# Ranking two experts with the router's tiles, searching for the other fourteen between weight tiles, and pinning the order of the expert units

## The chip, the cores and the metric

The kernel runs on one core of a Trainium2 chip. The metric is device microseconds (us) of one execution. Before the change the median of three runs is 1372.27 us (1369.42 to 1372.28).

## What is computed

One block of a hybrid diffusion transformer: 1024 latent tokens of width 1024 (and 256 context tokens that give a start state) go through a gated linear attention and a long convolution, and then through a mixture of experts in which each expert chooses its tokens. Only the last part is touched:

```
def _ec_moe(h, w_router, w_gate, w_up, w_down):      # 16 experts, cap = 128 tokens each
    aff = jax.nn.softmax((h @ w_router).astype(jnp.float32), axis=-1)
    vals, idx = lax.top_k(jnp.swapaxes(aff, 1, 2), cap)
    xs = h[bidx, idx]
    hid = jax.nn.silu(xs @ w_gate) * (xs @ w_up)      # per expert, 1024 x 1024 weights
    y = (hid @ w_down) * vals[..., None]
    return jnp.zeros_like(h).at[bidx, idx].add(y)
```

## The kernel before, in words

The program is one long function; a scheduling layer orders the instructions of each engine when the program is built, and each engine then runs its own list in that order. The stages up to the residual are not touched. The last two are:

**Router.** For each of the eight tiles of 128 tokens (tile 7 first, tile 0 last) the kernel finishes the attention output (`gla_out`), multiplies by the output weights (`residual`, matmuls into `pout`) and computes the 16 affinities (`router`: transposes `pth`, matmuls `plt`, softmax, the result in `aff`, line 1214). GpSimd (POOL) writes the tile to `d_acc` and the normed tile to `d_h`.

**Experts.** Each expert needs the places of its 128 best tokens. `select` (line 1273) finds the threshold by a search over the 30 bits of the affinity: a step makes candidate thresholds `thr` on VectorE (DVE), compares all affinities with them (`ge`, line 1309), lets TensorE (PE) count over the partitions (`psel`, line 1283, eight matmuls against a matrix of ones) and keeps the largest candidate with at least 128 tokens above it (lines 1314 and 1315). After the last step ties are resolved (`gt`, `eq`, `keep`) and `pos` holds each token's place. `select` is called twice: for experts 0 and 1 with 6 steps of 5 bits (names end in `a`), for experts 2 to 15 with 15 steps of 2 bits (names end in `b`). The second call is written behind `route(1)` and the scheduler spreads it over the first weight tiles.

`route(e)` (line 1347) turns places into token numbers: a one-hot `oh` on DVE, eight small matmuls into `pi`, a copy and an addition give `ix`, and POOL gathers the 128 rows of `d_h` into the single buffer `xs` (line 1362). `transposed` (line 1366) transposes those rows (`ptx` on PE), applies the norm's gain on ScalarE (ACT, `tt`) and splits them into a high and a low part, `thi` on ACT and `tlo` on DVE.

A **unit** is one 1024 x 1024 weight matrix: eight tiles `eraw` (or `erawl` for `w_down`), each split by ACT into `ehi` (line 144) and by DVE into `elo` (line 147), and each multiplied by six matmuls of 512 columns into `pex` (lines 150 to 152: high x high, low x high, high x low, for two halves). The units run gate 0, up 0, gate 1, down 0, up 1, gate 2, down 1 and so on. Expert e's gate ends with a silu on ACT (line 1385, `sg`), its up with a product on DVE (line 1406, `sg` again), its down with the scaled rows `y` on DVE (line 1417), which POOL adds into `d_acc`. `next_rows` transposes the next expert's rows and routes the one after it, behind tile 2 of an up unit (`KU`), and the hidden rows of the expert before are transposed behind tile 5 of a gate unit (`KB`); the scheduler may move all of these. The weight tiles are loaded by SyncE (SP) into 21 buffers for gate and up and 8 for down; `elo` has 4 buffers and `ehi` 5.

Of the kernel before, what the change touches and what calls it, by code (L numbers as in the profile page):

```python
# [42 lines left out]
def shape_constants():  # L43
# [45 lines left out]
    out["tokid"] = tid  # L89
    for b in (5, 2):  # L90
# [8 lines left out]
def tile_gla_hyena_moe(ctx: ExitStack, tc: tile.TileContext, io: dict, out: bass.AP):  # L99
# [49 lines left out]
    def mm3(out_, lh, ll, rh, rl, first, last):  # L149
        T.matmul(out_, lh, rh, start=first, stop=False)  # L150
        T.matmul(out_, lh, rl, start=False, stop=False)  # L151
        T.matmul(out_, ll, rh, start=False, stop=last)  # L152

# [821 lines left out]
    def gb(tag, bufs):  # L975
        return lambda shape, name: psg.tile(shape, F32, name=name, tag=tag, bufs=bufs)

    ga, gc, gd, ge1 = gb("ga", 2), gb("gc", 2), gb("gd", 1), gb("ge", 1)

# [119 lines left out]
    tokid = cload("tokid", [P, NT, 2], pool=keep)  # L1099
    digit = {b: cload(f"digit{b}", [P, 30 // b, 1 << b], I32, pool=keep) for b in (5, 2)}  # L1100
    ones = keep.tile([P, P], BF16, name="ones")
# [3 lines left out]
    SY.dma_start(befr, io["c_before"])  # L1105
    V.tensor_copy(before, befr)
    ws = [wout_tile(k, op_tile) for k in range(4)]
    p2a.close()
    g2 = p2.enter_context(tc.tile_pool(name="g2", bufs=1, side="right", reuse_waits="tile"))

    def h4(shape, name, tag, bufs, dt=F32):
        return g2.tile(shape, dt, name=name, tag=tag, bufs=bufs)


# [100 lines left out]

    outs, rows = [], []
    for i in reversed(range(-2 - 1, NT)):
        if i >= 0:
            outs.append((i, gla_out(i)))
        if rows:  # L1220
            router(*rows.pop(0))
        if outs and (i < 0 or len(outs) > 1):
            o_ = outs.pop(0)
            rows.append((o_[0], *residual(*o_)))
    p2.close()
    st_stack.close()
# [7 lines left out]
    def mt(shape, dt, name, tag, bufs):  # L1234
        return mp.tile(shape, dt, name=name, tag=tag, bufs=bufs)
# [5 lines left out]
    used = [0]  # L1241
    KB, KU = 5, 2
# [12 lines left out]

    loaded = {(w, k): expert_tile(w, 0, k) for w in ("w_gate", "w_up", "w_down") for k in range(KT)}

    def expert_mm(w, e, xt, between=None, at=KB):
        ps = pse.tile([P, D], F32, name="pex", tag="ex", bufs=3)
        for k in range(KT):  # L1260
            raw = loaded[w, k] if e == 0 else expert_tile(w, e, k)
            hi = mt([P, D], F32R, "ehi", "ehi", NHI)
            lo = mt([P, D], F32R, "elo", "elo", NLO)
            split(hi, lo, raw)
            for h in range(2):
                hs = slice(h * 512, (h + 1) * 512)
                mm3(ps[:, hs], xt[0][:, k], xt[1][:, k], hi[:, hs], lo[:, hs], k == 0, k == KT - 1)
            if between and k == at:
                between()
        return ps  # L1270

    pos = mp.tile([P, E, NT], BF16, name="pos")

    def select(e0, ne, tag, bits):
# [14 lines left out]

        if e0 == 0:  # L1290
            def pr(n):
                return pT([P, n], "psel")
        else:
            acc = pse.tile([P, D], F32, name="psel", tag="ex", bufs=3)
            flip = [0]

            def pr(n):
                flip[0] ^= 512
                return acc[:, flip[0]:flip[0] + n]

# [3 lines left out]
        for b in range(30 // bits):  # L1304
# [3 lines left out]
            ge = tl([P, nd - 1, ne, NT], BF16, "ge")  # L1308
            V.tensor_tensor(ge, aff_[:, None].to_broadcast([P, nd - 1, ne, NT]),
                            thr[:, 1:nd, :, None].to_broadcast([P, nd - 1, ne, NT]), op=ALU.is_ge)  # L1310
            pc = pr((nd - 1) * ne)
            column_sums(pc, ge.rearrange("p q e t -> p (q e) t"))
            upper = thr[:, 1:nd].rearrange("p q e -> p (q e)")
            V.scalar_tensor_tensor(upper, pc, float(CAP) - 0.5, upper, op0=ALU.is_ge, op1=ALU.mult)
# [6 lines left out]
        pg_ = pr(ne)  # L1321
        column_sums(pg_, gt)
        need = tl([P, ne], F32, "need")
        V.tensor_scalar(need, pg_, -1.0, float(CAP), op0=ALU.mult, op1=ALU.add)
# [9 lines left out]

    NF = 2
    select(0, NF, "a", 5)

# [10 lines left out]
    def route(e):  # L1348
        pi = pT([P, 5], "pi")
        oh = mt([P, NT, P], BF16, "oh", "s2", NS)  # L1350
        V.tensor_tensor(oh, slot[:, None, :].to_broadcast([P, NT, P]),
                        pos[:, e, :, None].to_broadcast([P, NT, P]), op=ALU.is_equal)
        for t in range(NT):
# [27 lines left out]

    def gate_part(e, xt, between=None):
        pg = expert_mm("w_gate", e, xt, between)
        sg = mt([P, D], F32, "sg", "sg", 1)
        A.activation(sg, pg, AF.Silu)
        return sg

    A.preload_act_table_set("silu_and_others")
    routed = [route(0)]
    xt = transposed(0, routed[0][2], True)  # L1390
    routed.append(route(1))
    select(NF, E - NF, "b", 2)
    with tc.issue_after(routed[0][3].ins):
        sg = gate_part(0, xt)
    m5 = row_of(5, mp)
    for e in range(E):
        ahead = []

        def next_rows():
            if e + 1 < E:  # L1400
                ahead.append(transposed(e + 1, routed[e + 1][2], True))
            if e + 2 < E:
                routed.append(route(e + 2))

        pu = expert_mm("w_up", e, xt, next_rows, KU)
        V.tensor_mul(sg, pu, sg)
        if e + 1 < E:
            sg_next = gate_part(e + 1, ahead[0], lambda: ahead.append(transposed(e, sg)))
        else:
            ahead = [None, transposed(e, sg)]  # L1410
        xt_next, ht = ahead
        py = expert_mm("w_down", e, ht)
        iv, ix = routed[e][0:2]
        if e + 1 == E:
            break
# [4 lines left out]
        xt, sg = xt_next, sg_next  # L1420

# [56 lines left out]
```

## Time and profile before

| | us |
|---|---|
| median of three runs | 1372.27 |
| profiled execution, its own time | 1373.86 |
| span of its trace | 1372.1 |
| PE busy in the span | 1277.9 (93%) |
| DVE busy | 1148.6 (84%) |
| ACT busy | 805.4 (59%) |
| expert matmuls into `pex`, number | 2304 |

The profile comes from one profiled execution, 1.59 us above the median; 1.76 us lie around its span. A row of a timeline has a start, a duration, the engine, the line of the kernel, the operation, the tile written and the tiles read; behind it, in brackets, the engine's idle time in front of it and what ended it. PEclk is the granted clock of TensorE as a share of full speed. A matmul's duration overlaps the next one's, so PE's pace is read from the distance of starts.

### The profile page before, as it was taken

Reading aid. Unit: us, or ns where it says so; the run is one execution under the profiler, and the core shown is the slowest. Engines: PE = TensorE matmul, PEld = TensorE weight load, DVE = VectorE, ACT = ScalarE, POOL = GpSimd, SP = SyncE. Lnnn points to the kernel's source line nnn. Section 1 sums busy time; section 2 is a strip of 40 time slices with the busy share of each in tenths; the row PEclk is TensorE's granted clock in tenths of the full one; section 3 lists DMA queues with packets and bytes.
Section 4 is the critical chain, followed back from the end, with each engine's and each line's share of the span. In section 5 each row is a group of like instructions: output and inputs, shape, how many; then the busy total and the mean of one; then the engine's idle time right before and its main releaser. Section 6 shows DMA issues by size and latency. Waiting matters only on the chain.

```text
span 1372.1 us, 21492 instructions
## 1 busy us (share of the span) xinstructions
PE 1277.9 (93%) x7721; PEld 1044.9 (76%) x7721; DVE 1148.6 (84%) x1913; ACT 805.4 (59%) x1226; POOL 126.8 (9%) x136
## 2 busy tenths in 40 slices
PE   6998999999999997998996899999999999999983
PEld 4788877787899896666774678888888888877762
DVE  7899549899767878788656799999999999988886
ACT  3285352211211315785563678888888888877864
POOL 1110000010110110001010000001111111012010
PEclk9999999999999997999996899999999999999996
DMA  8965442775565535666668789999999999999856
GB/s 268 342 195 172 139 108 77 229 187 183 142 201 151 141 113 177 168 159 191 242 227 326 251 322 357 361 393 382 388 389 384 388 389 386 370 374 364 279 184 245
DMA packets 143978, 354.81 MB, mean 259 GB/s; under 512 B 17925, under 2 KB 63629, under 8 KB 143615
## 3 DMA queue, kind: packets, MB, share of 16 engines
q1 hardware_dynamic: 124553, 293.88, 59.7%
q0 software_dynamic: 18928, 59.56, 15.8%
q8 instruction: 60, 0.98, 0.3%
q14 instruction: 47, 0.39, 0.1%
q10 hardware_dynamic: 390, 0.00, 0.0%
HBM read 310.89 MB, written 50.89 MB: 264 GB/s over the span
## 4 chain that ended last, share of the span: by engine, by line
PE 70%; issue 9%; DVE 8%; ACT 6%; DMA 5%; POOL 1%; POOLq 0%; SPq 0%; DVEq 0%; ACTq 0%
PE pex L151 13%; PE pex L152 12%; PE pex L150 12%; PE phy L565 3%; PE phy L563 3%; PE phy L562 3%; PE ptx L1372 2%; PE pdft L487 2%; DMA wt<-w_ada 2%; PE pdft L488 2%; PE pvg L150 2%; PE pvg L151 1%; PE pvg L152 1%; PE pm L351 1%; PE pdft L698 1%
## 5 line engine op out<-in xcount | busy, mean ns | idle before, releaser
L147 DVE TENSOR_TENSOR elo<-eraw,ehi 128x1024 fp32r<-128x1024 f32 x256 | 302.3, 1219 | 13.2 <-issue 6.0
L151 PE MATMUL pex<-elo,thi 128*128 128x512 f32 x768 | 306.0, 398 | 4.8 <-DVE elo L147 4.5
L150 PE MATMUL pex<-ehi,thi 128*128 128x512 f32 x768 | 305.4, 398 | 2.3 <-ACT thi L144 1.3
L152 PE MATMUL pex<-ehi,tlo 128*128 128x512 f32 x768 | 303.2, 395 | 0.8 <-DVE tlo L147 0.8
L144 ACT ACTIVATE ehi<-eraw 128x1024 fp32r<-128x1024 f32 x256 | 265.1, 1068 | 50.2 <-PE pex L152 48.2
L151 PEld LDWEIGHTS pex<-elo,thi 128*128 128x128 f32 x768 | 145.1, 189 | 40.6 <-DVE elo L147 10.7
L150 PEld LDWEIGHTS pex<-ehi,thi 128*128 128x128 f32 x768 | 145.3, 189 | 34.1 <-ACT thi L144 1.7
L152 PEld LDWEIGHTS pex<-ehi,tlo 128*128 128x128 f32 x768 | 145.1, 189 | 31.5 <-DVE tlo L147 1.2
L147 DVE TENSOR_TENSOR elo<-erawl,ehi 128x1024 fp32r<-128x1024 f32 x128 | 149.4, 1218 | 6.3 <-ACT ehi L144 5.5
L144 ACT ACTIVATE ehi<-erawl 128x1024 fp32r<-128x1024 f32 x128 | 131.4, 1057 | 19.7 <-PE pex L152 18.0
L144 ACT ACTIVATE whi<-wraw 128x1024 fp32r<-128x1024 f32 x30 | 31.7, 1058 | 116.5 <-PE pqk L563 28.8
L562 PE MATMUL phy<-xh,whi 128*128 128x512 f32 x192 | 76.7, 399 | 0.0
L563 PE MATMUL phy<-xl,whi 128*128 128x512 f32 x192 | 75.8, 395 | 0.0
L150 PE MATMUL pvg<-whi,xh 128*128 128x256 f32 x256 | 73.2, 286 | 0.0
L151 PE MATMUL pvg<-wlo,xh 128*128 128x256 f32 x256 | 72.4, 283 | 0.0
L152 PE MATMUL pvg<-whi,xl 128*128 128x256 f32 x256 | 72.4, 283 | 0.0
L1418 POOL DMA_INDIRECT d_acc<-y,ix x15 | 34.7, 2313 | 392.3 <-DVE y L1417 392.3
L1377 ACT ACTIVATE tt<-ptx,fcol,gfcol 128x128 f32<-128x128 f32 x128 | 48.7, 463 | 34.0 <-PE ptx L1372 34.0
L565 PE MATMUL phy<-xh,wlo 128*128 128x512 f32 x192 | 61.6, 398 | 1.0 <-DVE wlo L147 1.0
L458 ACT ACTIVATE D<-pdft 128x512 f32<-128x512 f32 x32 | 19.1, 597 | 69.5 <-PE pdft L488 39.0
L147 DVE TENSOR_TENSOR wlo<-wraw,whi 128x1024 fp32r<-128x1024 f32 x30 | 36.7, 1222 | 27.4 <-ACT whi L144 27.4
L487 PE MATMUL pdft<-kk,fmat 128*128 128x128 f32 x256 | 51.4, 283 | 3.2 <-ACT D L458 3.1
(459 smaller groups left out, 2596.2 us busy)
## 6 DMA issues: line engine op xcount, KB each, us to landing
eraw<-w_gate SPq DMA_DIRECT2D x128, 512.0 KB
eraw<-w_up SPq DMA_DIRECT2D x128, 512.0 KB
erawl<-w_down SPq DMA_DIRECT2D x128, 512.0 KB
wt<-w_ada SPq DMA_DIRECT2D x48, 512.0 KB
wraw<-w_in SPq DMA_DIRECT2D x30, 512.0 KB
kspec<-d_spec SPq DMA_DIRECT2D x16, 512.0 KB
xt<-x SPq DMA_DIRECT2D x8, 512.0 KB
d_spec<-ue POOLq DMA_DIRECT2D x8, 512.0 KB, 3.4
```

The source lines that it names most:

```text
L144: A.activation(hi, src, AF.Copy)
L147: V.tensor_sub(lo, src, hi.bitcast(F32))
L150: T.matmul(out_, lh, rh, start=first, stop=False)
L151: T.matmul(out_, lh, rl, start=False, stop=False)
L152: T.matmul(out_, ll, rh, start=False, stop=last)
L487: T.matmul(ps[:, r], fmat[:, r, m1], kk[m1 // 4][:, 0, m1 % 4], start=True, stop=False)
L488: T.matmul(ps[:, r], fneg[:, n1] if r else fmat[:, 0, n1], kk[n1 // 4][:, 1, n1 % 4], start=False, stop=True)
L562: T.matmul(ps[:, h], hi[:, k], rh[k][:, h], start=k == 0, stop=False)
L563: T.matmul(ps[:, h], hi[:, k], rl[k][:, h], start=False, stop=False)
L565: T.matmul(ps[:, h], lo[:, k], rh[k][:, h], start=False, stop=k == KT - 1)
L1377: A.activation(tt[:, k], pt[:, k], AF.Identity, bias=fcol[:, 0, kk_:kk_ + 1], scale=gfcol[:, kk_:kk_ + 1])
L1418: G.indirect_dma_start(out=d_acc[:, :], out_offset=bass.IndirectOffsetOnAxis(ap=ix[:, :1], axis=0), in_=y, in_offset=None, compute_op=ALU.add)
```

## The change

Experts 0 and 1 no longer have a search. As each router tile is done, `rank` transposes the affinities of an expert into a row (`prow`, copied to `arow`), counts on DVE how many tokens of the tiles done so far are above each token of this tile (`over`, with its sum in `cnt`, over 128 elements for tile 7 and up to 1024 for tile 0) and how many equal ones stand ahead (`tie`), and adds both to the rank `rk`. `rank_sums` takes the column sums of `over` on PE (`pbelow`, one small matmul for each tile done earlier) off the ranks of those tiles. At tile 0 the places `pos0` are read off. The rank of tile i is written one tile late, so that tile 1's and tile 0's follow each other; for tile 0, expert 1 comes behind the routing of expert 0.

The search for experts 2 to 15 is a generator that stops after each count. Three steps run ahead of the first unit, the rest are called behind weight tiles listed in `SEARCH_AT`; `route(2)` follows the last.

The units are one sequence: `split_ahead` issues the high parts four tiles and the low parts three tiles ahead of the matmuls, and everything else is put behind the splits and matmuls of its tile (`behind_splits`). The rows of the next expert are transposed behind tile 3 of an up unit, the routing comes behind tile 7, the hidden rows are transposed behind tile 2 of a gate unit. The first `w_down` is loaded by POOL behind the first gather, and the seven of the 21 buffers that lie in another pool are now taken last.

```diff
-        if (used[0] - 1) % (NR + NX) < NX:
+        if (used[0] - 1) % (NR + NX) >= NR:
...
+    def rank(i, experts, ptile, new):
+        W = (NT - i) * P
+        for e in experts:
+            row = ptile([P, P], name="prow")
+            T.transpose(row, aff[:, e, i:i + 1].to_broadcast([P, P]), ident)
+            V.tensor_copy(arow[e][:, i * P:(i + 1) * P], row)
+            a_ = aff[:, e, i:i + 1]
+            over = over2[e][:, i % 2]
+            cnt = tiny.tile([P, 2], F32, name="cnt")
+            V.tensor_scalar(over[:, 0:W], arow[e][:, i * P:], a_, 0.0, op0=ALU.is_gt, op1=ALU.add, accum_out=cnt[:, 0:1])
+            tie = new([P, P], BF16, name="tie")
+            V.scalar_tensor_tensor(tie, arow[e][:, i * P:(i + 1) * P], a_, after, op0=ALU.is_equal, op1=ALU.mult,
+                                   accum_out=cnt[:, 1:2])
+            V.scalar_tensor_tensor(rk[:, e, i:i + 1], cnt[:, 0:1], cnt[:, 1:2], rk[:, e, i:i + 1], op0=ALU.add, op1=ALU.add)
+            overs[e].append((e, i, over))
+            while len(overs[e]) > (i > 0):
+                rank_sums(*overs[e].pop(0), ptile)
+
+    def rank_sums(e, i, over, ptile):
+        if i + 1 < NT:
+            below = ptile([P, NT], name="pbelow")
+            for t in range(i + 1, NT):
+                T.matmul(below[:, t:t + 1], over[:, (t - i) * P:(t - i + 1) * P], ones[:, 0:1], start=True, stop=True)
+            V.tensor_sub(rk[:, e, i + 1:], rk[:, e, i + 1:], below[:, i + 1:])
+        if i == 0:
+            V.scalar_tensor_tensor(pos0[:, e], rk[:, e], CAP + 0.5, rk[:, e], op0=ALU.is_le, op1=ALU.mult)
...
-    select(0, NF, "a", 5)
...
+    def split_ahead(t):
+        while len(his) <= min(t + AH, len(stream) - 1):
...
+            last_split[0] = A.activation(hi, raw, AF.Copy)
...
+        while len(los) <= min(t + AL, len(stream) - 1):
...
+            last_split[1] = V.tensor_sub(lo, raw, hi.bitcast(F32))
...
+    def unit(j, xt, hooks):
+        ps = pse.tile([P, D], F32, name="pex", tag="ex", bufs=3)
+        for k in range(KT):
+            t = KT * j + k
+            split_ahead(t)
...
+            if k in hooks:
+                with behind_splits():
+                    hooks[k]()
...
+    SEARCH_AT = ((0, 1, 2, 4, 6), (0, 2, 5, 7), (1, 3, 5, 7), (0,))
+    search = select(NF, E - NF, "b", 2)
+    rank(0, [1], pT, lambda shape, dt, name: mt(shape, dt, name, "s2", NS))
+    with tc.issue_after(routed[0][4].ins):
+        loaded.update({("w_down", k): expert_tile("w_down", 0, k, G) for k in range(KT)})
...
+    for _ in range(3):
+        next(search)
...
+    def search_step():
+        if next(search, True):
+            routed.append(route(2))
```

Where the instructions now stand, engine by engine. First DVE at the end of the long search, up to the routing of expert 2 (`keepb` and `pos` close the search, `sg` is the product that waits for the end of an up unit, `oh`, `pv` and `ix` are the routing). Before, this lies among the splits of gate 1, and the product at the end of up 0 is long done:

```order
L1329 TENSOR_TENSOR keepb<-keepb,eqb 128x112
L147 TENSOR_TENSOR elo<-eraw,ehi 128x1024
L1330 TENSOR_TENSOR keepb<-keepb,gtb 128x112
L147 TENSOR_TENSOR elo<-eraw,ehi 128x1024
L1333 SCALAR_TENSOR_TENSOR pos<-psel,keepb 128x112
L147 TENSOR_TENSOR elo<-eraw,ehi 128x1024
L1351 TENSOR_TENSOR oh<-slot,pos 128x1024
```

and now, with 43 splits ahead of it, which is three tiles into gate 2:

```order
L1356 TENSOR_TENSOR keepb<-keepb,eqb 128x112
L1426 TENSOR_TENSOR elo<-eraw,ehi 128x1024
L1357 TENSOR_TENSOR keepb<-keepb,gtb 128x112
L1510 TENSOR_TENSOR sg<-pex,sg 128x1024
L1360 SCALAR_TENSOR_TENSOR pos<-psel,keepb 128x112
L1426 TENSOR_TENSOR elo<-eraw,ehi 128x1024
L1376 TENSOR_TENSOR oh<-slot,pos 128x1024
L1382 COPY pv<-pi 128x5
L1383 TENSOR_TENSOR ix<-pv 128x1
```

What moved: the routing of expert 2 stands behind the product of up 1 instead of ahead of it.

Second, PE where the rows of expert 2 are transposed (`ptx<-ident,xs`). Before, 210 expert matmuls (35 weight tiles) are ahead of it, and the eight matmuls `pi` of its routing stand 80 expert matmuls earlier:

```order
L152 MATMUL pex<-ehi,tlo 128x512
L1372 MATMUL ptx<-ident,xs 128x128 x8
L150 MATMUL pex<-ehi,thi 128x512
L151 MATMUL pex<-elo,thi 128x512
```

and now, with 240 expert matmuls (40 tiles, the end of up 1) ahead of it:

```order
L1379 LDWEIGHTS oh
L1379 MATMUL pi<-tv,oh 128x5
L1397 MATMUL ptx<-ident,xs 128x128 x8
L151 MATMUL pex<-ehi,thi 128x512
L152 MATMUL pex<-elo,thi 128x512
```

What moved: no expert matmul is left between the routing of expert 2 and the transposes of the rows that it gathers. The counts of the 12 search steps that are left for the units stand 3, 6, 9, 10, 13, 15, 18, 21, 24, 28, 32 and 35 whole tiles into the sequence, where `SEARCH_AT` calls the last of them 23 tiles in; the tie resolution follows at 38 to 40.

Third, DVE in every later expert, from an up unit's end to the hidden rows of the next gate unit. Before:

```order
L147 TENSOR_TENSOR elo<-eraw,ehi 128x1024
L147 TENSOR_TENSOR tlo<-tt,thi 128x512
L147 TENSOR_TENSOR elo<-eraw,ehi 128x1024
L1406 TENSOR_TENSOR sg<-pex,sg 128x1024
L147 TENSOR_TENSOR elo<-eraw,ehi 128x1024 x6
L147 TENSOR_TENSOR elo<-erawl,ehi 128x1024 x2
L147 TENSOR_TENSOR tlo<-ptx,thi 128x512 x2
```

and now:

```order
L148 TENSOR_TENSOR tlo<-tt,thi 128x512
L1426 TENSOR_TENSOR elo<-eraw,ehi 128x1024
L1376 TENSOR_TENSOR oh<-slot,pos 128x1024
L1510 TENSOR_TENSOR sg<-pex,sg 128x1024
L1382 COPY pv<-pi 128x5
L1426 TENSOR_TENSOR elo<-eraw,ehi 128x1024
L1383 TENSOR_TENSOR ix<-pv 128x1
L1385 TENSOR_REDUCE iv<-pv 128x1
L1426 TENSOR_TENSOR elo<-eraw,ehi 128x1024 x2
L148 TENSOR_TENSOR tlo<-ptx,thi 128x512 x2
```

What moved: three splits instead of eight lie between the product and the hidden rows' low parts, and the one-hot stands directly ahead of the product.

## Rows read from the trace of the kernel before

**Rows 1.** Windows: stretch and its length, then busy time of each engine, PEclk, DMA.

```profile
726.50:731.50 5.00, 1.83 (x22) 1.05 (x23) 1.69 (x12) 4.45 (x11) 1.04 (x2) 0.85 1.03 418
726.00:763.00 37.00, 17.56 (x185) 14.78 (x183) 26.30 (x93) 11.11 (x21) 2.34 (x3) 0.55 0.77 305
842.00:1195.00 353.00, 352.93 (x1683) 288.53 (x1682) 339.36 (x341) 302.60 (x369) 36.51 (x20) 1.00 1.01 383
1195.00:1310.00 115.00, 110.96 (x500) 87.25 (x499) 101.42 (x99) 88.09 (x111) 14.71 (x5) 0.99 0.87 317
```

**Rows 2.** Timeline of ACT: the silu at the end of gates 2, 12 and 15.

```profile
842.29 1.03 ACT L1385 ACTIVATE sg<-pex 128x1024 f32<-128x1024 f32 x1 [0.34 <-PE pex L152]
...
1195.14 1.03 ACT L1385 ACTIVATE sg<-pex 128x1024 f32<-128x1024 f32 x1 [0.31 <-PE pex L152]
...
1309.61 1.03 ACT L1385 ACTIVATE sg<-pex 128x1024 f32<-128x1024 f32 x1 [2.70 <-PE pex L152]
```

**Rows 3.** Timeline of DVE: last affinities, and places of experts 0 and 1.

```profile
731.23 0.29 DVE L1214 TENSOR_SCALAR aff<-ex,sm 128x16 f32<-128x16 f32 x1
...
751.29 0.17 DVE L1333 SCALAR_TENSOR_TENSOR pos<-psel,keepa 128x16 bf16<-128x16 f32 x1
```

**Rows 4.** Timeline of POOL: the gather for expert 0.

```profile
754.42 1.27 POOL L1362 DMA_INDIRECT xs<-d_h,ix  x1 [22.89 <-PE psel L1283]
```

**Rows 5.** Timeline of PE: the first expert matmuls.

```profile
759.74 1.94 PE L1372 MATMUL ptx<-ident,xs 128*128 128x128 f32 x8 [5.73 <-DMA xs<-d_h,ix]
...
764.59 0.77 PE L152 MATMUL pex<-ehi,tlo 128*128 128x512 f32 x1
765.16 0.63 PE L150 MATMUL pex<-ehi,thi 128*128 128x512 f32 x1
...
766.44 0.63 PE L150 MATMUL pex<-ehi,thi 128*128 128x512 f32 x1
...
768.05 0.40 PE L150 MATMUL pex<-ehi,thi 128*128 128x512 f32 x1
...
772.25 0.77 PE L1283 MATMUL psel<-geb,ones 128*128 128x42 bf16 x8
772.82 0.48 PE L150 MATMUL pex<-ehi,thi 128*128 128x512 f32 x1
```

**Rows 6.** DVE groups by form: a scalar operation on 512 elements.

```profile
L246 DVE TENSOR_SCALAR sn<-sy 128x512 f32<-128x512 f32 x2 | 0.8, 422 | 0.0
```

**Rows 7.** Timeline of PE: transposes of a router tile, and one routing.

```profile
699.27 1.09 PE L1197 MATMUL pth<-ident,xres 128*128 128x128 f32 x8
...
801.89 0.36 PE L1354 MATMUL pi<-tv,oh 128*128 128x5 bf16 x8
```

**Rows 8.** DVE groups by form, 900 to 1000 us.

```profile
L147 DVE TENSOR_TENSOR elo<-eraw,ehi 128x1024 fp32r<-128x1024 f32 x46 | 54.4, 1220 | 2.6 <-issue 1.2 <-PE pex L151 0.7
...
L147 DVE TENSOR_TENSOR tlo<-ptx,thi 128x512 fp32r<-128x512 f32 x6 | 3.8, 679 | 0.0
...
L1406 DVE TENSOR_TENSOR sg<-pex,sg 128x1024 f32<-128x1024 f32 x3 | 3.7, 1219 | 0.0
```

**Rows 9.** Timeline of DVE: the product at the end of up 1.

```profile
830.65 1.21 DVE L1406 TENSOR_TENSOR sg<-pex,sg 128x1024 f32<-128x1024 f32 x1
```

**Rows 10.** The tile xs: all sixteen gathers, from issue to landing.

```profile
DMA to landing us min/median/max: 4.7/8.1/12.7
```

**Rows 11.** Timeline of DVE around the product at the end of an up unit.

```profile
1074.51 1.23 DVE L147 TENSOR_TENSOR elo<-eraw,ehi 128x1024 fp32r<-128x1024 f32 x1
1075.65 0.68 DVE L147 TENSOR_TENSOR tlo<-tt,thi 128x512 fp32r<-128x512 f32 x1
1076.25 1.22 DVE L147 TENSOR_TENSOR elo<-eraw,ehi 128x1024 fp32r<-128x1024 f32 x1
1077.42 1.23 DVE L1406 TENSOR_TENSOR sg<-pex,sg 128x1024 f32<-128x1024 f32 x1
```

More of the change, by code (lines that the diff above doesn't have):

```diff
@@ L83, in shape_constants @@
     out["before"] = (ss < cc).astype(f)
+    out["after"] = (ss > cc).astype(f)
     out["slot"] = np.broadcast_to(np.arange(1, P + 1, dtype=f), (P, P)).copy()
@@ L151, in mm3 @@
         T.matmul(out_, lh, rl, start=False, stop=False)
-        T.matmul(out_, ll, rh, start=False, stop=last)
+        return T.matmul(out_, ll, rh, start=False, stop=last)
     def rsqrt(dst, ssum, n, width, fused=False):
@@ L1099, in tile_gla_hyena_moe @@
     tokid = cload("tokid", [P, NT, 2], pool=keep)
-    digit = {b: cload(f"digit{b}", [P, 30 // b, 1 << b], I32, pool=keep) for b in (5, 2)}
+    digit = {b: cload(f"digit{b}", [P, 30 // b, 1 << b], I32, pool=keep) for b in (2,)}
     ones = keep.tile([P, P], BF16, name="ones")
@@ L1106, in tile_gla_hyena_moe @@
     V.tensor_copy(before, befr)
+    after = keep.tile([P, P], F32, name="after")
+    SY.dma_start(after, io["c_after"])
+    pos0 = keep.tile([P, NF, NT], BF16, name="pos0")
+    rk = keep.tile([P, NF, NT], F32, name="rk")
+    V.tensor_scalar(rk, tokid[:, None, :, 1].to_broadcast([P, NF, NT]), 1.0, None, op0=ALU.add)
     ws = [wout_tile(k, op_tile) for k in range(4)]
@@ L1112, in h4 @@
         return g2.tile(shape, dt, name=name, tag=tag, bufs=bufs)
+    arow = [g2.tile([P, L], F32, name="arow0"), mid_tile("arow1")]
+    over2 = [mid.tile([P, 2, L], BF16, name="over", tag="x", bufs=NX) for _ in range(NF)]
     diag = [g2.tile([P, NH, P], F32, name=f"diag{x}") for x in range(2)]
@@ L1220, in tile_gla_hyena_moe @@
         if rows:
+            ranks.append(rows[0][0])
             router(*rows.pop(0))
@@ L1224, in tile_gla_hyena_moe @@
             rows.append((o_[0], *residual(*o_)))
+        while len(ranks) > 1 or ranks == [0]:
+            rank(ranks[0], range(NF if ranks[0] else 1), gc, s2)
+            ranks.pop(0)
     p2.close()
@@ L1254, in expert_tile @@
         return raw
[L1256 to L1270, printed above, removed]
+    loaded = {(w, k): expert_tile(w, 0, k) for w in ("w_gate", "w_up") for k in range(KT)}
     pos = mp.tile([P, E, NT], BF16, name="pos")
@@ L1380, in transposed @@
         return hi, lo
[L1382 to L1386, printed above, removed]
+    units = [("w_gate", 0)]
+    for e in range(E):
+        units += [("w_up", e)] + ([("w_gate", e + 1)] if e + 1 < E else []) + [("w_down", e)]
+    stream = [(w, e, k) for w, e in units for k in range(KT)]
+    AH, AL = NHI - 1, NLO - 1
+    his, los, last_split = [], [], [None, None, None]
@@ new lines, in behind_splits @@
+    def behind_splits():
+        stack = ExitStack()
+        for x in last_split:
+            stack.enter_context(tc.issue_after(x.ins))
+        return stack
+    def unit(j, xt, hooks):
[3 more added lines that the diff above has]
+            split_ahead(t)
+            for h in range(2):
+                hs = slice(h * 512, (h + 1) * 512)
+                last_split[2] = mm3(ps[:, hs], xt[0][:, k], xt[1][:, k], his[t][0][:, hs], los[t][:, hs], k == 0, k == KT - 1)
+            if k in hooks:
+                with behind_splits():
+                    hooks[k]()
+        return ps
@@ L1393, in tile_gla_hyena_moe @@
-    with tc.issue_after(routed[0][3].ins):
-        sg = gate_part(0, xt)
+    for _ in range(3):
+        next(search)
     m5 = row_of(5, mp)
[L1396 to L1412, printed above, removed]
+    sgs, hts = {}, {}
```

79 lines of the change are left out of this document (59 added, 20 removed).

## The prediction

> **What bounds it now.** I read the windows first. From 842 to 1195 us PE is busy 352.9 of 353 us at full clock, DVE 96% [rows 1]: the experts are bound by PE. The silu at a gate's end marks a period: ten experts from 842.29 to 1195.14 take 35.3 us each, the last three up to 1309.61 take 114.5, that is 8.6 more than three regular ones [rows 2]. The reader should see PE at 111 of 115 us there, and DMA below 1 [rows 1]. The second place with idle PE is the border between router and experts: 17.6 of 37 us busy, granted clock 0.55 [rows 1]. There the chain runs from the last affinities at 731.5 through the first search to the places at 751.3 [rows 3], the gather at 754.4 [rows 4], its rows at 759.7, and full work from 764.6, when the first low part of the rows is there [rows 5]. So two gains are in reach: some 20 us of search at the border, and 8.6 us at the irregular end.
>
> **Prices.** PE: between 768.05 and 772.25 lie 18 expert matmuls, 0.233 us each, a tile of six 1.40; a count of the search takes 0.57 (772.25 to 772.82); at the lower clock a matmul takes 0.43 (three from 765.16 to 766.44) [rows 5]. A transpose is 0.11 to 0.14 and eight routing matmuls 0.36 [rows 7]. DVE: a split takes 1.22 by itself and 1.13 to 1.14 in a row of splits [rows 11], a `tlo` 0.6 to 0.68, a product 1.22 [rows 8].
>
> **1. Router stage: 5.9 us later.** Of the 16 `prow` transposes and 56 `pbelow` matmuls, 10 and 12 stand ahead of the last `pout`: about 1.5 us of PE that was full there; I take 2. More costly is DVE. The ranks of tiles 2 and 1 stand between the links of tile 0's own chain (norm, softmax), for two experts each: four `over` of 768 or 896 elements, four copies, four `tie` and eight additions. `over` with its sum is in no row. Its floor is the scalar operation on 512 elements, 0.42 [rows 6], its ceiling a whole 1024-element product, 1.22 [rows 8]; I take 1.0, twice the floor for twice the elements plus a short instruction to read the sum. That makes 4 + 0.8 + 1 + 1.4 = 7.2 us. DVE is idle 3.3 of the 5 us of that chain [rows 1], so 3.9 stick out (2 to 6 with the bounds). The affinities end at 737.4.
>
> The Trainium skill (VectorE: DVE Perf Modes, The perf-mode tier table) says that scalar operations on fp32 in SBUF run at twice the rate of those on two tensors. The trace agrees for one without a sum: 0.42 [rows 6] against 0.68 on 512 elements [rows 8]. By that rule `over` would be some 0.6 and this term some 1.6 us shorter, an estimate; no run here shows it with a sum.
>
> **2. Border: PE starts 4.8 us earlier.** The first search, 19.8 us from affinities to places, goes. In its place stand a transpose, a copy, one `over` of 1024, a `tie`, seven `pbelow`, additions and two casts, 4.1 us: places at 741.5. From places to gather it was 3.1 us; now the count of the long search's first step stands on PE ahead of `pi`, and the comparison for it behind `oh` on DVE, and the copy for expert 1 stands between `pv` and `ix`: 5.8, gather at 747.3, 7.1 us earlier. The rows took 5.3 to come and should again, since the prefetched weights have landed by then (range 4.7 to 12.7 [rows 10]): 752.6. Then DVE is what is late: behind the first transpose stands a count, and behind that the third step and four splits, before `tlo` may run: 752.6 + 2 + 4 x 1.135 + 0.6 = 759.8, against 764.6.
>
> **3. Up to the end of up 1: 2.2 us earlier.** From there 238 matmuls (55.6), 12 counts (6.8), the tie resolution (1.4), 16 transposes (1.7), the low clock at the start (2.0) and 1.1 of small waits make 68.6: up 1 ends at 828.4. Before, its product began at 830.65 [rows 9]. DVE holds: 39 splits are 44.3 of the 68.6, and 24 are left for 12 steps and six other operations.
>
> **4. Expert 2 waits for its rows: 16.7 us.** On PE nothing is left between routing and transposes of expert 2. Once up 1 has ended, DVE still has the end of `keep` and a split (1.6), the product (1.15), `pos` (0.2), a split (1.15) and `oh` (1.2): 833.7. Routing matmuls, copy, addition and the issue take 1.9, the rows 5.3 and the way to the first `tlo` 4.85 (759.74 to 764.59 [rows 5]), less 0.5 for two matmuls that go ahead. Gate 2 starts at 845.3 instead of 830.6, 14.7 later, and PE, idle that long, restarts at the low clock as at the border [rows 5], 2.0 more. Nothing covers it: gate 2's own splits run ahead only as far as their buffers, and down 1 is behind gate 2.
>
> **5. The regular end: 8.4 us less.** Thirteen experts from gate 2 to gate 15 took 467.3 us [rows 2]; at 35.3 they take 458.9. The pinned order repeats exactly, so the irregular end goes.
>
> **6. The pinned order's own price: 7.8 us.** Before, the split that the first gate tile needs is done at 1075.74, 1.7 us before the product shows the end of up [rows 11]. After that `tlo`, product and, eight splits later, two `tlo` (2.9 us) cost less than the 0.26 us that DVE gains on PE with each split. Now `oh` comes there too, and the two `tlo` follow after three splits: 4.4 us, regained by five splits (1.3) and PE's own pauses for routing and transposes (1.1). That leaves DVE 0.3 late by the lead of 1.7; with the lead of 1.4 that ACT's later `ehi` allows, 0.6. I take 0.6 x 13; bounds 0 and 1.0, so 0 to 13 us.
>
> **7. Tail: 1 us less.** One split instead of two stands ahead of the last hidden rows' `tlo`. The rest (last tiles of `w_down`, final norm) is as before. The other edits, the order of the buffers and POOL's loads of the first `w_down`, I cost at nothing: these tiles are wanted 24 tiles after the start. If that cover went, a late tile would show as PE waiting for `erawl`.
>
> **Sum.** 16.7 - 8.4 + 7.8 - 1.0 = +15.1 (terms 1 to 3 are inside 16.7). The profiled execution's 1373.86 becomes 1389; it stood 1.6 above the median, so the median goes from 1372.3 to **1387 us**.
>
> **Rivals.**
> - *Interleaving pays* (faster). The wait for expert 2 does not appear, because DVE finishes the search well ahead of PE. Then -2.2 - 8.4 + 0 - 1 gives about 1360, down to 1358. For it: the search is called behind tiles up to 24, and both gains are real in the rows. Against: each engine runs its list, and in the list 43 splits and a product that waits for up 1 are ahead of `pos`. It decides itself at one place: whether `pos` can come before up 1 ends. The Trainium skill (Perfetto Trace Analysis, Optimization Strategy) says that interleaving regimes with different bounds may help; by that rule the search between tiles would be a gain. Before, the search already lies between tiles, and its routing is 80 matmuls ahead of the transposes. Chance 0.11.
> - *The wait comes, the pinned order is free.* Term 6 is 0 and terms 1 to 4 are some us better: 1376 to 1381. For it: DVE's slack is a matter of tenths. Chance 0.22.
> - *The gather is slow.* At 12.7 us instead of 5.3 [rows 10] the wait grows by 7: 1394 to 1398. For it: in the experts DMA's share is 1.01 [rows 1]. Against: when PE waits, buffers are full and loads stop. Chance 0.11.
> - *It comes out even.* Wait of 9 or 10 us and the 8.4 regained: 1372. It needs the start and the wait both better than worked out. Chance 0.08.
>
> **Numbers.** My forecast, between 1381 and 1394, has 0.48. Slower are it, the free order and the slow gather, 0.81; 0.2% is 2.7 us, about what a measurement of this kernel can tell; even 0.08; faster 0.11. The range 1373 to 1397 leaves the faster rival and the ends out.
>
> **What would show it.** Right: the last affinities at 736 to 739, first expert gather near 747, full expert matmuls from 760; PE idle by 12 to 17 us between up 1 and gate 2, with the gather of expert 2 issued some 7 us after up 1's end and the clock halved; then gates 35.3 to 36.3 us apart to the last. Wrong: `pos` done before up 1 ends, a period below 35.3, or PE waiting for weight tiles.

## The result, and the profile after

The changed kernel takes 1380.87 us (median of 6 runs, 1377.45 to 1383.60), the kernel before 1372.06 us (6 runs, 1369.28 to 1372.28): 8.8 us slower, ratio 1.0063 with a 95% interval of 1.0045 to 1.0082. The forecast was 1387 with a range of 1373 to 1397. The profiled execution took 1381.33 us with a span of 1379.6, 7.5 above the span before. One execution of the kernel of experiment 2 took 6990.33 us and is left out of its numbers.

The windows of the changed kernel (columns as in [rows 1]) show one stretch that was full before and is not now, 830 to 850 us, at a granted clock of 0.59; PE works 7.8 of its 20 us. From there to gate 15 it is full again (119.6 of the last 120 us), where before it lost 4 of 115.

```profile
830.00:850.00 20.00, 7.83 (x43) 5.94 (x43) 8.73 (x16) 5.33 (x12) 2.27 (x2) 0.59 0.53 200
850.00:1200.00 350.00, 348.51 (x1655) 284.27 (x1654) 329.02 (x330) 297.69 (x364) 45.19 (x19) 1.00 1.00 371
1200.00:1320.00 120.00, 119.55 (x569) 97.57 (x568) 113.09 (x115) 103.20 (x126) 14.11 (x6) 1.00 0.94 357
```

The timeline of ACT, the silu at the end of a gate, answers to [rows 2]: gate 0, gate 1, gate 2, gate 3, and the last two. Gate 2 is 55.95 us behind gate 1 (before 35.78), gate 3 is 35.73 behind gate 2, each later one 35.5 and the last 34.22; the last three no longer stand out.

```profile
776.35 1.02 ACT L1469 ACTIVATE sg<-pex 128x1024 f32<-128x1024 f32 x1
803.93 1.02 ACT L1469 ACTIVATE sg<-pex 128x1024 f32<-128x1024 f32 x1 [0.29 <-PE pex L153]
859.88 1.03 ACT L1469 ACTIVATE sg<-pex 128x1024 f32<-128x1024 f32 x1 [0.30 <-PE pex L153]
895.61 1.03 ACT L1469 ACTIVATE sg<-pex 128x1024 f32<-128x1024 f32 x1 [0.25 <-PE pex L153]
...
1286.25 1.03 ACT L1469 ACTIVATE sg<-pex 128x1024 f32<-128x1024 f32 x1 [0.28 <-PE pex L153]
1320.47 1.03 ACT L1469 ACTIVATE sg<-pex 128x1024 f32<-128x1024 f32 x1 [0.25 <-PE pex L153]
```

The timeline of DVE around the end of up 1 (829 us) and of PE behind it show why. DVE's list has the product and a split ahead of the places of experts 2 to 15 (`pos`), and another split ahead of the one-hot. PE's last matmul of up 1 starts at 828.73 (828.4 was forecast as its end), the routing at 834.35, the transposes at 841.37, gate 2 at 844.95. Its second matmul follows 0.59 us later, and the next ones go on at about 0.43 us each up to 850. The granted clock is 0.94 from 829 to 834 us, where PE works 0.56 of the 5 us, and 0.50, the lower of its two levels (1.2 and 2.4 GHz), from 834 to 850.

```profile
830.63 1.22 DVE L1510 TENSOR_TENSOR sg<-pex,sg 128x1024 f32<-128x1024 f32 x1
831.76 0.26 DVE L1360 SCALAR_TENSOR_TENSOR pos<-psel,keepb 128x112 bf16<-128x112 f32 x1
831.95 1.22 DVE L1426 TENSOR_TENSOR elo<-eraw,ehi 128x1024 fp32r<-128x1024 f32 x1
833.08 1.22 DVE L1376 TENSOR_TENSOR oh<-slot,pos 128x1024 bf16<-128x1024 bf16 x1
```

```profile
828.73 0.40 PE L153 MATMUL pex<-ehi,tlo 128*128 128x512 f32 x1
...
834.35 0.38 PE L1379 MATMUL pi<-tv,oh 128*128 128x5 bf16 x8 [3.15 <-DVE oh L1376]
841.37 1.97 PE L1397 MATMUL ptx<-ident,xs 128*128 128x128 f32 x8 [6.65 <-DMA xs<-d_h,ix]
844.95 0.79 PE L151 MATMUL pex<-ehi,thi 128*128 128x512 f32 x1 [1.61 <-ACT thi L145]
```

The first stages, up to the first router tile, are the same in both kernels but for a few small setups, and they do not take the same time in each execution: the first affinities come at 666.67 before and at 664.72 after, and between 660.2 and 666.0 in the profiles of the experiments. So the stretches are measured from there. Timeline of DVE before, and after (first affinities, two comparisons of a rank, last affinities, comparison over 1024 elements):

```profile
666.67 0.24 DVE L1214 TENSOR_SCALAR aff<-ex,sm 128x16 f32<-128x16 f32 x1
```

```profile
664.72 0.24 DVE L1225 TENSOR_SCALAR aff<-ex,sm 128x16 f32<-128x16 f32 x1
...
729.20 1.01 DVE L1238 TENSOR_SCALAR_CACHE_REDUCE over<-arow,aff 128x768 bf16<-128x768 f32 x1
...
734.82 1.15 DVE L1238 TENSOR_SCALAR_CACHE_REDUCE over<-arow,aff 128x896 bf16<-128x896 f32 x1
...
739.18 0.24 DVE L1225 TENSOR_SCALAR aff<-ex,sm 128x16 f32<-128x16 f32 x1
...
740.32 1.28 DVE L1238 TENSOR_SCALAR_CACHE_REDUCE over<-arow,aff 128x1024 bf16<-128x1024 f32 x1
```

PE's first matmul on a low part of expert 0's rows came at 764.59 before [rows 5]; its timeline after:

```profile
761.08 0.80 PE L153 MATMUL pex<-ehi,tlo 128*128 128x512 f32 x1 [2.16 <-DVE tlo L148]
```

With these and the silu rows, the 7.5 us divide like this; the forecast's terms are put into the same stretches.

| stretch | before | after | difference | forecast |
|---|---|---|---|---|
| start to first affinities | 666.67 | 664.72 | -1.95 | 0 |
| first to last affinities (term 1) | 64.56 | 74.46 | +9.90 | +5.9 |
| to the first low-part matmul (term 2) | 33.36 | 21.90 | -11.46 | -10.7 |
| to the silu of gate 2 (terms 3, 4) | 77.70 | 98.80 | +21.10 | +21.5 |
| gate 2 to gate 15 (terms 5, 6) | 467.32 | 460.59 | -6.73 | -0.6 |
| gate 15 to the end (term 7) | 62.49 | 59.13 | -3.36 | -1.0 |
| span | 1372.1 | 1379.6 | +7.5 | +15.1 |

### The profile page after: what moved, and what is told of

It reads as the page before. It is cut to its first block, busy times and chain, and to the rows that moved or that the text cites. A ratio compares the mean times of both kernels' runs of the same rounds, so it can differ in the third digit from the quotient of the medians.

```text
span 1379.6 us, 21577 instructions
## 1 busy us (share of the span) xinstructions
PE 1277.3 (93%) x7721; PEld 1043.6 (76%) x7721; DVE 1158.7 (84%) x1994; ACT 810.1 (59%) x1226; POOL 138.8 (10%) x144
## 3 DMA queue, kind: packets, MB, share of 16 engines
q0 software_dynamic: 20080, 63.75, 16.6%
## 4 chain that ended last, share of the span: by engine, by line
PE 44%; DVE 5%; DMA 2%; ACT 1%; issue 1%; POOLq 0%; DVEq 0%
PE pex L152 13%; PE pex L153 12%; PE pex L151 12%; PE ptx L1397 2%; DVE elo L1426 1%; DMA eraw<-w_gate 1%; PE pout L151 1%; PE pout L153 1%; PE pout L152 1%; DVE xf L1538 1%; PE psel L1312 1%; DVE over L1238 1%; DVE state L659 0%; DMA xs<-d_h,ix 0%; PE pi L1379 0%
## 5 line engine op out<-in xcount | busy, mean ns | idle before, releaser
L151 PE MATMUL pex<-ehi,thi 128*128 128x512 f32 x768 | 301.6, 395 | 2.9 <-ACT thi L145 2.9
L1387 POOL DMA_INDIRECT xs<-d_h,ix x16 | 34.2, 2140 | 209.2 <-PE ptx L1397 169.0
```

Of the source, the lines that this page charges most:

```text
L1387: gather = G.indirect_dma_start(out=xs_, out_offset=None, in_=d_h[:, :], in_offset=bass.IndirectOffsetOnAxis(ap=ix[:, :1], axis=0))
```

## The experiments

The columns between ratio and the last are differences of starts in the timelines: last minus first affinities, then to the silu of gate 0, to that of gate 2, to that of gate 15. The ratio is to the kernel before, run on the same chip, with its 95% interval. On those chips the kernel before took 1371.96 (experiments 1, 2, 3 and 5), 1374.04 (6 to 9) and 1371.51 (4 and 10), so medians from different chips can be compared only to some 2 us.

| kernel | median us | ratio | router | gate 0 | gate 2 | gate 15 |
|---|---|---|---|---|---|---|
| before | 1372.06 | | 64.56 | 47.75 | 63.31 | 467.32 |
| the change | 1380.87 | 1.0063 (1.0045 to 1.0082) | 74.46 | 37.17 | 83.53 | 460.59 |
| five steps first | 1372.28 | 0.9996 (0.9981 to 1.0012) | 74.40 | 41.59 | 69.31 | 460.88 |
| rows not waiting | 1364.29 | 0.9949 (0.9934 to 0.9964) | 74.45 | 37.11 | 67.31 | 460.55 |
| hidden behind 5 | 1387.16 | 1.0128 (1.0108 to 1.0148) | 74.42 | 37.40 | 83.60 | 466.49 |
| routing behind 4 | 1375.60 | 1.0035 (1.0023 to 1.0047) | 74.44 | 36.89 | 83.53 | 454.94 |
| pinned alone | 1363.84 | 0.9931 (0.9914 to 0.9948) | 64.58 | 50.96 | 61.67 | 460.84 |
| pinned, routing behind 4 | 1358.68 | 0.9894 (0.9874 to 0.9913) | 64.57 | 50.55 | 60.54 | 456.80 |
| six steps, routing behind 4 | 1366.36 | 0.9946 (0.9929 to 0.9964) | 74.42 | 44.04 | 63.29 | 456.48 |
| the same, ranks late | 1362.14 | 0.9917 (0.9897 to 0.9938) | 69.92 | 45.36 | 63.29 | 456.45 |
| pinned, splits behind route | 1358.79 | 0.9901 (0.9882 to 0.9920) | 64.56 | 49.62 | 62.39 | 456.86 |
| hidden behind 3 | 1384.25 (one execution) | | 74.54 | 37.38 | 81.85 | 466.52 |

**1. Rows that do not wait.**

```diff
-(pos0[:, e] if e < NF else pos[:, e])
+(pos0[:, 0] if e == 2 else pos0[:, e] if e < NF else pos[:, e])
...
-        if next(search, True):
-            routed.append(route(2))
+        next(search, True)
...
+            if e == 0:
+                hooks[6] = lambda: routed.append(route(2))
```

> The search stays in the experts, but the rows of expert 2 no longer hang on it: they are fetched in up 0 with the places of expert 0 (this kernel leaves out expert 2's own places). Theory (the loss is the wait): no idle stretch ahead of gate 2, its silu at 841 to 846 us, median 1363 to 1367. Rival (the search's own work is the loss): silu of gate 2 within 4 us of 859.9, median 1376 or more.

Measured: 1364.29, 16.6 us below the change, with the same 14 pieces of the search still between the weight tiles; their `pos` comes at 827.10, and PE does not wait for it. From gate 0 to gate 2 it takes 67.31 instead of 83.53. The loss is the wait, and not the search's work on DVE. ACT's timeline, gates 0 and 2:

```profile
774.37 1.02 ACT L1469 ACTIVATE sg<-pex 128x1024 f32<-128x1024 f32 x1
...
841.68 1.03 ACT L1469 ACTIVATE sg<-pex 128x1024 f32<-128x1024 f32 x1 [0.25 <-PE pex L153]
```

**2. Five steps of the search ahead of the units.**

```diff
-    SEARCH_AT = ((0, 1, 2, 4, 6), (0, 2, 5, 7), (1, 3, 5, 7), (0,))
+    SEARCH_AT = ((0, 1, 2, 4, 6), (0, 2, 5, 7), (1, 3, 5))
...
-    for _ in range(3):
+    for _ in range(5):
         next(search)
```

> Five steps of the long search, not three, stand ahead of the first unit, and its last pieces two tiles earlier, so the routing of expert 2 stands 31 tiles into the list of TensorE and no longer at tile 40, behind up 1. Theory (the loss is the wait for expert 2's rows): the idle stretch of 15.8 us between up 1 and gate 2 goes, and the 2 us of low clock with it; the two steps ahead of the first full matmul cost 0 to 5 us, since its low part is waited for anyway. The silu of gate 2 comes at 843 to 847 us instead of 859.9, the median falls from 1380.9 to 1364 to 1369. Rival (the search's 24 us of VectorE are the loss, wherever they stand): the same work delays splits instead, the silu of gate 2 stays within 4 us of 859.9 and the median at 1376 or more.

Measured: 1372.28, level with the kernel before and 8.6 us below the change, but above the 1364 to 1369 of the theory. With two more steps ahead (and the last calls two tiles earlier) the last count of the search stands 22 whole tiles into PE's list instead of 35. PE's timeline shows both prices that were put too low. The two steps stand behind the first matmul and hold DVE, so that its first low part comes at 764.82 (gate 0's silu 4.4 us later than in the change); and the rows of expert 2, though their routing stands 31 tiles in, ahead of up 1, still come 3.48 us late.

```profile
756.89 0.80 PE L151 MATMUL pex<-ehi,thi 128*128 128x512 f32 x1 [0.99 <-ACT thi L145]
757.49 0.81 PE L1312 MATMUL psel<-geb,ones 128*128 128x42 bf16 x8
759.67 0.77 PE L1312 MATMUL psel<-geb,ones 128*128 128x42 bf16 x8 [1.37 <-DVE geb L1334]
...
764.82 0.79 PE L153 MATMUL pex<-ehi,tlo 128*128 128x512 f32 x1 [3.21 <-DVE tlo L148]
...
828.82 1.24 PE L1397 MATMUL ptx<-ident,xs 128*128 128x128 f32 x8 [3.48 <-DMA xs<-d_h,ix]
```

**3. Hidden rows behind tile 5.**

```diff
-            hooks[2] = lambda: hidden(e - 1)
+            hooks[5 if e > 1 else 2] = lambda: hidden(e - 1)
```

> The transposes of the hidden rows stand behind tile 5 of a gate unit, as before the change, not behind tile 2 (from expert 2 on): five splits instead of two or three between the product and their low parts. Theory (the extra 0.25 us of an expert is VectorE being late where the one-hot comparison, the product and two low parts come together): from gate 3 on the period falls from 35.53 to 35.25 to 35.35 us, 12 periods give 2 to 3.5 us, median 1377.5 to 1379. Rival (the extra is TensorE's own list or the transposes' place is not what counts): period 35.5, median within 1 us of 1380.9.

Measured: 1387.16, 6.3 us slower than the change, with a period of 35.97. Both theories fail. PE's timeline shows a new wait of 0.71 us at the first split behind the product, four us ahead of the transposes (the waits count 13 such, 8.9 us in all).

```profile
1065.41 0.49 PE L152 MATMUL pex<-elo,thi 128*128 128x512 f32 x1 [0.71 <-DVE elo L1426]
...
1069.42 1.03 PE L1397 MATMUL ptx<-ident,sg 128*128 128x128 f32 x8
```

In the change the transposes stand exactly there, 0.89 us from their start to the next matmul, and that matmul follows without a wait that the trace would name:

```profile
1064.72 1.03 PE L1397 MATMUL ptx<-ident,sg 128*128 128x128 f32 x8
1065.61 0.50 PE L152 MATMUL pex<-elo,thi 128*128 128x512 f32 x1
```

So the transposes were cover, on this reading: PE did work that needs no split while DVE made the late one.

**4. Hidden rows behind tile 3**, to test that reading (the same line, with 3 for 5).

> The transposes of the hidden rows behind tile 3 of a gate unit, not tile 2 (from expert 2 on). Theory formed on the run with tile 5, where the period rose to 35.97 (right behind the product TensorE has no split left, and the 0.9 us of the transposes, if they stand there, cover that): behind tile 3 they stand five matmuls too late, TensorE waits some 0.7 us for the first split behind the product, period 35.8 to 36.0. Rival (what counts is the number of splits between product and the two low parts, the fewer the better): one split more, period 35.55 to 35.75, without a wait at the product.

One profiled execution: period 35.97, and the same wait of 0.71 us, now five matmuls ahead of the transposes. Four splits between product and low parts here and six in the run before made no difference; the change has three, and there another split is late (term 6 below). PE's timeline:

```profile
1062.49 0.50 PE L152 MATMUL pex<-elo,thi 128*128 128x512 f32 x1 [0.71 <-DVE elo L1426]
1063.74 1.03 PE L1397 MATMUL ptx<-ident,sg 128*128 128x128 f32 x8
```

**5. Routing behind tile 4.**

```diff
-                hooks[7] = lambda: routed.append(route(e + 2))
+                hooks[4] = lambda: routed.append(route(e + 2))
```

> The routing of the expert after next stands behind tile 4 of an up unit, not behind tile 7, so its one-hot comparison comes ahead of the low parts and away from the product. Theory (the extra 0.25 us of an expert is VectorE being late where comparison, product and two low parts come together): period 35.53 to 35.25 to 35.35 us, median 1377.5 to 1379. Rival (it is the three splits between product and hidden rows alone): period 35.5, median within 1 us of 1380.9.

Measured: 1375.60, 5.3 us below the change, period 34.95, further down than expected and below the 35.28 of the kernel before too. DVE's one-hot (1049.40) now comes five us ahead of the product (1054.39), and PE has no pause left in the regular experts beyond those for transposes and routing (the last two gates stand 35.69 and 34.79 apart). Timelines of DVE, and of ACT for two gates:

```profile
1049.40 1.22 DVE L1376 TENSOR_TENSOR oh<-slot,pos 128x1024 bf16<-128x1024 bf16 x1
...
1054.39 1.22 DVE L1510 TENSOR_TENSOR sg<-pex,sg 128x1024 f32<-128x1024 f32 x1
```

```profile
1029.85 1.03 ACT L1469 ACTIVATE sg<-pex 128x1024 f32<-128x1024 f32 x1 [0.24 <-PE pex L153]
...
1064.79 1.03 ACT L1469 ACTIVATE sg<-pex 128x1024 f32<-128x1024 f32 x1 [0.25 <-PE pex L153]
```

**6. The pinned sequence alone.** The units of the change with the two searches of the kernel before; the second is written out ahead of the units and `route(2)` comes in up 0. The order of the buffers and SP's loads of the first `w_down` are those of before too.

```diff
+    for _ in select(0, NF, "a", 5):
+        pass
...
-        while len(ranks) > 1 or ranks == [0]:
-            rank(ranks[0], range(NF if ranks[0] else 1), gc, s2)
-            ranks.pop(0)
...
-    SEARCH_AT = ((0, 1, 2, 4, 6), (0, 2, 5, 7), (1, 3, 5, 7), (0,))
+    SEARCH_AT = ()
...
+    held = begun[0]
+    for _ in search:
+        pass
...
-            if 0 < e < E - 2:
+            if e < E - 2:
```

> The pinned sequence alone: experts 0 and 1 are searched for ahead of the experts as before the change, the long search is written out ahead of the units, and no ranks are taken. Theory (the ranks are a net loss: from the first router tile's affinities to the last 74.5 us instead of 64.6, and from the last affinities to the silu of gate 2, wait removed, 104.4 instead of 111.1, so +3.3 together; the gain is the regular end): gate 2 comes as before the change, gates 2 to 15 take 460.6 instead of 467.3 us and the rest 59 instead of 62.5, median 1360 to 1364. Rival (the ranks are what gains at the border, and the pinned units alone start no earlier or lose their lead to the search): 1367 to 1374.

Measured: 1363.84, 0.69% faster than before. From the first affinities to the end of the span it takes 697.9 us, against 705.4 before and 714.8 in the change. The gain of the change is its pinned order, and the ranks with the search between the tiles are its loss; the buffers and the loads of `w_down` were not taken by themselves. The ranks and the search between the tiles, with the wait taken away, were put at 3.3 us and cost 1.7: from the first affinities to the silu of gate 2 it is 177.2 us here and 178.9 in experiment 1. ACT's timeline, gates 0 and 2:

```profile
779.71 1.03 ACT L1463 ACTIVATE sg<-pex 128x1024 f32<-128x1024 f32 x1
...
841.38 1.03 ACT L1463 ACTIVATE sg<-pex 128x1024 f32<-128x1024 f32 x1 [0.25 <-PE pex L152]
```

**7. The same with the routing behind tile 4** (the edit of experiment 5).

> As the pinned sequence alone, and the routing of the expert after next behind tile 4 of an up unit instead of tile 7. Theory (the two gains are of different places and add up): period 34.9 to 35.0 us, 12 times 0.55 us below the 1362 expected without it, median 1353.5 to 1357.5. Rival (what the routing's place gains at one border is lost where the two low parts of the rows come later): within 2 us of the pinned sequence alone.

Measured: 1358.68, 1.2 us above the forecast, ratio 0.9894: with experiment 10 the fastest here, faster than both kernels. In its window of regular experts PE is busy 349.8 of 350 us. The period is 34.95 but for the last three, 36.12, 36.14 and 34.81, and so gates 2 to 15 gained 4.0 us on experiment 6 and not 6.6. In the first two of them DVE stands idle for the routing matmuls, with the next split behind them in its list, and PE then waits for that split. A window of regular experts, and the timelines of DVE and PE behind it:

```profile
845.00:1195.00 350.00, 349.83 (x1684) 288.45 (x1683) 337.92 (x341) 303.64 (x371) 37.33 (x20) 1.00 1.02 386
```

```profile
1213.34 0.17 DVE L1378 COPY pv<-pi 128x5 f32<-128x5 f32 x1 [2.31 <-PE pi L1375]
...
1214.95 0.50 PE L151 MATMUL pex<-elo,thi 128*128 128x512 f32 x1 [0.63 <-DVE elo L1422]
```

**8. Six steps first, routing behind tile 4**, with the ranks kept: `range(6)`, `SEARCH_AT = ((0, 1, 2, 4, 6), (0, 2, 5, 7), (1, 3))` and the edit of experiment 5.

> The changed kernel with six steps of the search ahead of the first unit, not three, the last pieces up to tile 19, and the routing behind tile 4. Theory (in the run with five steps the rows of expert 2 still came 3.5 us late and the two steps held the first full matmul 3.7 us; six steps end the first and cost some 2.5 us more at the start): no wait ahead of gate 2, silu of gate 2 some 120 us behind its last affinities less 14, that is 106 to 110, period 34.95, median 1360 to 1365. Rival (the wait moves but stays): PE idle over 3 us ahead of gate 2, median 1367 or more.

Measured: 1366.36, 1.4 us above the range of the theory. The wait ahead of gate 2 is gone (63.29 us from gate 0, as before the change), but the three steps put gate 0 6.9 us later. Steps ahead of the units cost 2.2 to 2.3 us each (experiment 2 and this one).

**9. Ranks late**, otherwise as experiment 8.

```diff
-        while len(ranks) > 1 or ranks == [0]:
-            rank(ranks[0], range(NF if ranks[0] else 1), gc, s2)
+        while ranks and (ranks[-1] == 0 or len(ranks) > 1 and ranks[0] > 2):
+            rank(ranks[0], range(NF if ranks[0] > 2 else 1), gc, s2)
...
-    rank(0, [1], pT, lambda shape, dt, name: mt(shape, dt, name, "s2", NS))
+    for i in (2, 1, 0):
+        rank(i, [1], pT, lambda shape, dt, name: mt(shape, dt, name, "s2", NS))
```

> As the run with six steps and the routing behind tile 4, with the ranks of router tiles 2 and 1 taken behind the affinities of tile 0 for expert 1, and for expert 0 only as VectorE comes to them. Theory (the ranks of these tiles stand between the links of tile 0's own chain): from the first tile's affinities to the last 66 to 72 us instead of 74.4, 2 to 5 us back behind them for the later places, median 1 to 4 us below the run without it. Rival (TensorE's order sets the router, the ranks on VectorE are beside it): 74.4 us stay, median the same or higher.

Measured: 1362.14. The router takes 69.92 instead of 74.42 us, 1.3 come back behind it, and the median falls by 4.2. The ranks of two tiles did hold the chain of the last tile: its link, from tile 1's affinities to its own, falls from 10.44 to 5.93 us, and the links before it stay. Even so the kernel is 3.5 us slower than experiment 7, which has no ranks. DVE's timeline, first and last affinities:

```profile
664.60 0.24 DVE L1225 TENSOR_SCALAR aff<-ex,sm 128x16 f32<-128x16 f32 x1
...
734.52 0.24 DVE L1225 TENSOR_SCALAR aff<-ex,sm 128x16 f32<-128x16 f32 x1
```

**10. Splits behind the first routing**, otherwise as experiment 7.

```diff
-            with tc.issue_after(held.ins):
+            with tc.issue_after(routed[0][3].ins):
```

> As the pinned sequence alone with the routing behind tile 4, but the first four splits stand behind the indices of expert 0, as before the change, not between the links of its search. Theory (each split between two links of the first search holds that chain): from the last affinities to the silu of gate 0 47 to 48.5 us instead of 50.5, later parts as in that run, median 2 to 3.5 us below its 1358.7. Rival (the splits filled time in which the chain waited for TensorE anyway, and now delay the first matmul instead): 50 us or more, median the same.

Measured: 1358.79, no change. The gather does leave earlier, 24.1 us behind the last affinities instead of 26.3, but PE then waits 5.75 us for the rows (1.27 in experiment 7, where steps of the search fill that time), and of the 2.3 us 0.9 are left at gate 0; at gate 2 0.9 is lost. PE's timeline:

```profile
757.44 1.97 PE L1393 MATMUL ptx<-ident,xs 128*128 128x128 f32 x8 [5.75 <-DMA xs<-d_h,ix]
```

## Why the prediction was right, and where it was off

**Terms 3 and 4 held**, and they decide the sign. The place named was "whether `pos` can come before up 1 ends"; it came at 831.76, behind the product. The one-hot was to be done at 833.7 and was at 834.3, and gate 2 started at 844.95 against 845.3. That so little is missing is luck in part: the first stages came 1.95 us earlier than before, and term 1 was too small (below); counted from the first affinities, the silu of gate 2 came 2.8 us later than forecast. That the wait is the cause is shown by experiment 1, which keeps the search between the tiles and only routes expert 2 in up 0. The rival "interleaving pays" fell: the routing of expert 2 stands 40 weight tiles into PE's list, where before it stood 22 tiles in, and so the end of the search became the bound. The Trainium skill (Perfetto Trace Analysis, Optimization Strategy) says that interleaving regimes may help. Here it gave no gain: with the wait 1380.87 us, without it 1364.29, and 1363.84 with no ranks and most of the search ahead of the units (experiment 6).

The wait has a cause further back that the prediction does not name: the first search had covered part of the long one. PE's timelines show nine of the long search's fifteen counts ahead of the first expert matmul before, among those of the first search, eleven in experiment 6, and three in the change. So the places of experts 2 to 15 came at 798.93 before and 789.68 in experiment 6, against 831.76 in the change; with six steps written ahead of the units (experiment 8) they come at 812.86, and the wait is gone. Timelines of DVE, before and in experiment 6:

```profile
798.93 0.26 DVE L1333 SCALAR_TENSOR_TENSOR pos<-psel,keepb 128x112 bf16<-128x112 f32 x1
```

```profile
789.68 0.27 DVE L1352 SCALAR_TENSOR_TENSOR pos<-psel,keepb 128x112 bf16<-128x112 f32 x1
```

**Term 1 was too small by 4 us.** The step that failed is that only "the ranks of tiles 2 and 1", "between the links of tile 0's own chain", were priced on DVE. They do cost there: tile 0's link (from tile 1's affinities to its own) grew by 3.15 us where 3.9 were taken, and experiment 9, without those ranks there, gives 4.5 back. But tile 1's link grew by 2.2 and tile 2's by 3.75, each with the ranks of earlier tiles in it, and that was not counted; the four links before those grew by 0.8 together. `over` was taken at 1.0 and measured 1.01, 1.15 and 1.28 on 768, 896 and 1024 elements. By the tier table that the prediction weighed (the Trainium skill, VectorE: DVE Perf Modes, The perf-mode tier table) it would have been about half of that, an estimate. Another sentence of the Trainium skill (SBUF — State Buffer, Who interferes with whom) leaves out of the faster modes that use two ports "the form that also writes out its accumulator". The trace agrees: 1.28 us on 1024 elements with a sum, 0.42 on 512 without [rows 6].

**Term 6 was too large, and is the largest miss.** 0.6 us an expert were taken; the period rose from 35.28 to 35.51, that is 0.23. With the last, shorter period (34.22) gates 2 to 15 took 460.6 where the forecast had 458.9 + 7.8. The cluster is where it was said to be, and its price was nearly right: with the one-hot away from it (experiment 5) the period is 34.95, 0.56 less than in the change. In the change 0.09 of that stands at the transposes, and most of the rest at a matmul 5.6 us behind them. Timelines of PE and DVE:

```profile
1069.60 0.61 PE L151 MATMUL pex<-ehi,thi 128*128 128x512 f32 x2
1070.35 0.50 PE L152 MATMUL pex<-elo,thi 128*128 128x512 f32 x1
```

```profile
1067.88 1.28 DVE L148 TENSOR_TENSOR tlo<-ptx,thi 128x512 fp32r<-128x512 f32 x2
1069.08 2.35 DVE L1426 TENSOR_TENSOR elo<-eraw,ehi 128x1024 fp32r<-128x1024 f32 x2
```

The last matmul stands 0.75 us behind the first of the two ahead of it, where two regular steps are 0.45: its split follows the two low parts and comes 0.30 late. What was mis-sized is the base. The period of 35.28 before, to which 0.6 was added, was itself 0.33 above 34.95: in two of its periods (from 1018.6 to 1089.2 us) the distances of PE's matmuls, those at transposes and routing left out, sum to 0.55 and 0.28 us more than at 0.227 each, and in two of the change to 0.07 and 0.10. The prediction's pace came from such a slower stretch too, 0.233 us a matmul, where undisturbed it is 0.227 (1058.79 to 1062.87 in the change, 18 matmuls, 4.08 us). What holds PE there no row names. The faster pace alone would have made the term larger, since DVE gains 0.22 us and not 0.26 with each split. Where PE's own pauses stand counts too: experiments 3 and 4 move the transposes away from the late split and lose 0.46 us an expert.

**Term 5 held**: the last three experts take their regular time. **Term 7** was 1.0 and came to 3.4: the irregular end before went on through up 15, whose product comes 23.85 us behind gate 15's silu there and 21.76 now. Timeline of DVE, the product of up 15 before and after:

```profile
1333.46 1.23 DVE L1406 TENSOR_TENSOR sg<-pex,sg 128x1024 f32<-128x1024 f32 x1 [1.78 <-PE pex L152]
```

```profile
1342.23 1.22 DVE L1510 TENSOR_TENSOR sg<-pex,sg 128x1024 f32<-128x1024 f32 x1 [0.30 <-PE pex L153]
```

The measured time lies where the forecast's own range (1381 to 1394) meets that of the rival in which the pinned order is free (1376 to 1381), and by mechanism it is between them: the wait came in full, and the order cost 1.7 us in all instead of 7.8. The last period, 34.22, is below the 35.3 that was named as a sign of being wrong; no other period is. Misses of both signs partly cancel in the total: of the 7.6 us between forecast and trace, 6.1 are terms 5 and 6, 2.4 term 7, 2.0 the spread of the first stages, less 2.8 of terms 1 to 4.

## What to carry to other kernels

Between tiles of a stage with one full engine, a serial search is not free: each of its steps waits for its turn in an in-order list (with twelve counts between the tiles its places came at 831.76 us, with four at 789.68), so reckon when its last result is out and who stands behind that. Before taking a chain away, ask what ran beside it. Put PE work that needs no new split (here the transposes) right where the splits are late, and keep long operations of the splitting engine apart from each other. Try the parts of a change alone: counted from the first affinities, here one part was worth 7.5 us, and the rest cost 17.

## What the runs showed that was not expected

- Moving eight transposes one to three tiles on costs 0.46 us an expert; whether four or six splits lie between product and low parts, which was thought to matter, does not show.
- The comparison with a sum takes 1.28 us on 1024 elements, as long as an operation on two tensors.
- First stages that are the same but for small setups end anywhere between 660.2 and 666.7 us in twelve profiles; differences of a few us between kernels are to be read from the first stage that they change.
